# Decoder step on one core: the bias copies of heads 4 to 7 tied to attention's first four stores instead of the sixth projection chunk's

## The chip, the cores and the metric

The kernel runs on one core of one Trainium2 chip. The metric is the device time of one execution in microseconds (us). The engines are TensorE (PE, with its weight loads shown as PEld), VectorE (DVE), ScalarE (ACT), GpSimd (POOL) and SyncE (SP, which here only issues transfers).

## The reference

One inference step of a hybrid decoder: a state-space branch beside sparse attention with a relative-position bias, then a mixture of 32 experts of which each token takes four. There are 1024 prompt tokens and eight sample tokens, the latter with a paged cache of 4096 positions each. The part around the change is attention:

```python
def nsa_core(q, gates, q_pos, ckv, gather_fn, n_blocks, wkv, w_pos, table):
    ...
    o_cmp, p_cmp = attend_compressed(qh, ckv, q_pos, table)
    idx, valid = select_blocks(p_cmp, q_pos, n_blocks)
    o_sel = attend_selected(qh, gather_fn(idx), idx, valid, q_pos, table)
    o_win = attend_window(qh, wkv, q_pos, w_pos, table)
    ...
    g = jax.nn.sigmoid(gates.astype(F32)).astype(o.dtype)
    return jnp.einsum('bqhdr,bqhr->bqhd', o, g).reshape(B, Tq, D_ATT)
```

Each of the three branches adds to its scores a bias that depends on the head and on the distance of query and key only (`shared_bias`: `table[rel_bucket(dist)]`), and takes a softmax. A query block is 128 prompt tokens; eight heads share two key/value heads, four to each.

## The kernel before

**Stages.** `run` (L2293) goes through adaLN, preparation of the state-space branch and the bias, then `mixer_x` (normalised input), `mixer` (input projection with the state-space branch beside it), `attention`, `post` (output projection, router), `dispatch`, `experts` and `combine`. All weights are split into a high and a low part, so a product is three matmuls (L476 to L478).

**Projection.** `mixer` loads `w_in` in seven chunks of columns (a = 0, 256, 512, 768, 1024, 1280, 1536). For each, `w_split` (L622) loads raw weights into `wir` (L631, by SP, three buffers), ACT makes the high part `wih` (L632) and DVE the low part `wil` (L633); then come the eight sample rows and the eight token tiles t. Chunk 1024 stores `cmp_p`, chunk 1280 stores `sel_p` (both eight stores of `kv` by SP), chunk 1536 makes the windowed keys, values and gates and stores the last four tiles to `win_p` (L729).

**Bias.** `bias_prep` (L1258) leaves in DRAM the tile `bt`, 8 heads by 1152 distances. `spread_bias` copies one row of `bt` to 128 rows of `bx`, DRAM to DRAM, 576 KB for each head, issued by SP. `tc.issue_after(x)` makes the scheduler place it behind instruction x. Attention reads `bx` with a row step of 1151 elements, which gives each query row its own shift: the table `tt` (L1346), four transfers for a group of four heads, one buffer.

**Attention.** `attention` (L1319) runs over group g = 0, 1 (heads 0 to 3, then 4 to 7), for each over the eight query blocks t, up in g = 0 and down in g = 1. `soft` makes the scores of four heads into `sc` on PE (L1366 to L1383), DVE adds the bias and takes the row maximum (L1360), ACT makes the exponentials (L1390), DVE and ACT scale them (L1399, L1397). `values` transposes (L1413), splits (`th` L1416 on ACT, `tl` L1417 on DVE) and multiplies by the values (L1418, L1419) into `po`, which has one buffer; at the end DVE adds the halves into `at` (L1428, L1429) and SP stores it to `attd` (L1430). The values of one block are interleaved with the scores of the next.

**Sample chain.** The eight sample tokens' attention is a generator, `self.chain`, of which `block` takes about one step per block of values, tied with `issue_after` to that block's matmul `last`. Its first part, `sample_prep` (L1466), loads rows `hdn` (L1532), multiplies (L1534), makes compressed probabilities `pc` (L1539), picks the 15 best blocks and ends in the row numbers `rx` (L1600). Its second part, `sample_attention` (L1644), fetches cache rows `slab` by `rx` (L1661, POOL, two buffers), 16 fetches in four groups n of four. Each fetch is copied (`kw` L1668, `sv` L1679 on POOL), transposed (L1682), copied on ACT (`kt` L1687), multiplied (L1690) and added to its bias (`st` L1692 on DVE). Four of them make a group: transposed (L1697), copied to `px` (L1699), put through a softmax (L1637 to L1642, ACT L1639), transposed again (L1707, L1708) and multiplied by `sv` (L1716). `sv` and `px` have one buffer.

**What sets the order.** The Tile scheduler orders all instructions of an engine at build time, by dependencies, by the `issue_after` ties and by its own reckoning of when engines and transfers are free. On the chip each engine works through its list in that order.

Of the kernel before, what the change touches and what calls it, by code (L numbers as in the profile page):

```python
# [451 lines left out]
class K:  # L452
# [192 lines left out]
    def mixer(self, ctx):  # L645
        nc, i, o = self.nc, self.i, self.o
# [8 lines left out]
        with ExitStack() as c:  # L655
            side, early = (c.enter_context(ExitStack()) for _ in range(2))
            self.wir = self.pool("wir", ctx=early)
            self.wi[1] = self.pool("wi1", ctx=early)
            q = self.pool("miq", bufs=2, psum=True, ctx=c)
            for m, (a, n) in enumerate(((0, 256), (256, 256), (512, 256), (768, 256), (1024, 256), (1280, 256), (1536, 280))):  # L660
                hi, lo = self.w_split(self.wi[m % 2], win[:, a:a + n], n, "wi", 1, self.wir) if m else self.w0
                if a == 256:
                    steps = self.ssm(side)
                if a == 1280:
                    for _ in steps:
                        pass
                    side.close()
                    kv = self.pool("kv", ctx=ctx, side="right")
                    self.kh = kv.tile([128, 2, 2, T], FR, name="kh")
                    self.kl = kv.tile([128, 2, 2, T], FR, name="kl")  # L670
                    self.v = kv.tile([128, 2, 2, NT, 128], FR, name="v")
                if a == 1536:
                    early.close()
                    self.late = ctx.enter_context(ExitStack())
                    self.sap = self.pool("sap", ctx=self.late, side="right")
                    self.compress_prompt()
                def sample_rows():
                    po = q.tile([128, 512], F, name="po")
                    self.proj(po[:8, :n], slice(T, T + B), hi, lo, n)
                    zt = p2.tile([8, 280], F, name="zt")  # L680
                    nc.scalar.activation(out=zt[:, :n], in_=po[:8, :n], func=AF.Copy)
                    nc.sync.dma_start(out=self.zs[:, a:a + n], in_=zt[:, :n])
                    if a >= 1280:
                        nc.sync.dma_start(out=self.vnew[:, :, int(a == 1536)], in_=zt[:, 128:256].rearrange("b (h d) -> b h d", h=2))
                    if a in (1024, 1280):
                        nc.sync.dma_start(out=o["cmp_s" if a == 1024 else "sel_s"][0].rearrange("b t c h d -> (b t) (c h d)"), in_=zt[:, :256])
                    if a == 1536:
                        nc.sync.dma_start(out=self.zg, in_=zt[:, 256:280])
                        nc.sync.dma_start(out=o["win_s"][0].rearrange(wst)[:, 511], in_=zt[:, :256])
                if m:  # L690
                    sample_rows()
                for t in range(NT):
                    if 256 <= a < 1280 and t % 2:
                        next(steps, None)
                    po = q.tile([128, 512], F, name="po")
                    self.proj(po[:, :n], slice(t * 128, (t + 1) * 128), hi, lo, n)
                    rows = slice(t * 128, (t + 1) * 128)
                    flat = "o t c h d -> (o t) (c h d)"
                    if a < 512:
                        ut = p2.tile([128, 256], F, name="kv")  # L700
                        nc.scalar.activation(out=ut, in_=po[:, :256], func=AF.Copy)
                        nc.sync.dma_start(out=self.ud.rearrange("m t f -> (m t) f")[rows, a:a + 256], in_=ut)
                    elif a < 1024:
                        g = (a - 512) // 256
                        qd = p2.tile([128, 4, 2, 64], F, name="qd")
                        nc.scalar.activation(out=qd, in_=po[:, :256].rearrange("p (h d) -> p h d", h=4)[:, :, None, :].to_broadcast([128, 4, 2, 64]), func=AF.Copy, scale=0.125)
                        tp = q.tile([128, 4, 128], F, name="tp")
                        for h in range(4):
                            nc.tensor.transpose(tp[:, h], qd[:, h].rearrange("p a d -> p (a d)"), self.ident)
                        dst = self.qs[:, g * 4:g * 4 + 4, rows]  # L710
                        nc.scalar.activation(out=dst, in_=tp, func=AF.Copy)
                        nc.vector.tensor_tensor(out=dst[64:128], in0=tp[64:128], in1=dst[64:128].bitcast(F), op=ALU.subtract)
                    else:
                        if a > 1024:
                            kd = p2.tile([128, 2, 2, 64], F, name="qd")
                            nc.scalar.activation(out=kd, in_=po[:, 0:128].rearrange("p (h d) -> p h d", h=2)[:, :, None, :].to_broadcast([128, 2, 2, 64]), func=AF.Copy)
                        kv = p2.tile([128, 280], F, name="kv")
                        nc.scalar.activation(out=kv[:, :n], in_=po[:, :n], func=AF.Copy)
                        if a == 1024:
                            st = nc.sync.dma_start(out=o["cmp_p"][0].rearrange(flat)[rows], in_=kv[:, :256])  # L720
                            self.spread_bias(st, a, t)
                            continue
                        br = int(a == 1536)
                        if br == 0:
                            st = nc.sync.dma_start(out=o["sel_p"][0].rearrange(flat)[rows], in_=kv[:, :256])
                            self.spread_bias(st, a, t)
                        else:
                            if t >= 4:
                                nc.sync.dma_start(out=o["win_p"][0].rearrange(flat)[(t - 4) * 128:(t - 3) * 128], in_=kv[:, :256])  # L729
                            gv, kg = self.gate[:, t].rearrange("p (h r) -> p h r", r=3), kv[:, 256:280].rearrange("p (h r) -> p h r", r=3)  # L730
                            nc.vector.tensor_copy(out=gv[:, :, 0:2], in_=kg[:, :, 1:3])
                            nc.vector.tensor_copy(out=gv[:, :, 2:3], in_=kg[:, :, 0:1])
                        tp = q.tile([128, 4, 128], F, name="tp")
                        for h in range(2):
                            nc.tensor.transpose(tp[:, h], kd[:, h].rearrange("p a d -> p (a d)"), self.ident)
                        nc.scalar.activation(out=self.kh[:, br, :, rows], in_=tp[:, :2], func=AF.Copy)
                        nc.vector.tensor_tensor(out=self.kl[:, br, :, rows], in0=tp[:, :2], in1=self.kh[:, br, :, rows].bitcast(F), op=ALU.subtract)
                        v32 = kv[:, 128:256].rearrange("p (h d) -> p h d", h=2)
                        nc.vector.tensor_copy(out=self.v[:, br, :, t, 0:64], in_=v32)
                        nc.gpsimd.tensor_tensor(out=self.v[:, br, :, t, 64:128], in0=v32, in1=self.v[:, br, :, t, 0:64].bitcast(F), op=ALU.subtract)  # L740
                if not m:
                    sample_rows()
            self.chain = self.sample()
            next(self.chain)
            nc.scalar.activation(out=self.gate, in_=self.gate, func=AF.Sigmoid)

    def spread_bias(self, st, a, t):

        if t % 2:
            h = (a - 1024) // 64 + t // 2  # L750
            with self.tc.issue_after(st.ins):
                self.nc.sync.dma_start(out=self.bx[h:h + 1], in_=self.bt[h:h + 1, None].to_broadcast([1, 128, 1152]))


    def exp_poly(self, pool, out, x, n):
# [563 lines left out]
    def attention(self):  # L1319
        nc = self.nc  # L1320
        v, A, pe = nc.vector, nc.scalar, nc.tensor
        self.att = self.tc.dram_tile([128, 4, T], F, name="attd")
        with ExitStack() as c:
# [78 lines left out]
            def values(g, t, pr):  # L1402
                nonlocal last
                rows = slice(t * 128, (t + 1) * 128)
# [23 lines left out]
                v.tensor_tensor(out=at[lo], in0=ov[lo, :, 0], in1=sh[lo], op=ALU.add)  # L1428
                v.tensor_tensor(out=at[hi], in0=ov[hi, :, 1], in1=sh[hi], op=ALU.add)  # L1429
                self.put = nc.sync.dma_start(out=self.att[:, 2 * g:2 * g + 2, rows], in_=at).ins  # L1430

# [951 lines left out]
```

## Time and profile before

| | |
|---|---|
| median of three runs | 3181.55 us (3177.50 to 3199.51) |
| profiled execution | 3182.16 us, span 3180.5 us, mean granted PE clock 0.95 |
| PE, PEld busy | 93%, 75% of the span |
| DVE, ACT, POOL busy | 73%, 56%, 11% of the span |
| chunk 1280 and 1536 of the projection | about 578 to 655 us |
| attention | about 655 to 1067 us |

The rows shown below give the start of an instruction in us from the start of the span, its length, the engine, line and tiles, and in square brackets how long the engine was idle before it and what released it. "SPq" is an issue of a transfer by SP. A matmul is told by its records: a start to the next start is what it cost, and a wider spacing at the same shape is a lower clock. "Granted clock" (PEclk) is the share of 2.4 GHz that TensorE got.

### The profile page before, as it was taken

The page shows a single profiled execution, that of the slowest core. Times are in us where ns is not written, and L with a number is a line of the kernel's source. Part 1 is how long each engine was busy: PE and PEld are TensorE (multiplying, and loading weights), DVE is VectorE, ACT ScalarE, POOL GpSimd, SP SyncE. Part 2 cuts the span into 40 slices and gives each one's busy share as a digit, 9 for nine tenths or more (in the row PEclk, how much of TensorE's full clock was granted, in tenths as well). Part 3 has the DMA queues.
Part 4 walks back from the last instruction along what each step waited for, and adds up shares of the span by engine and source line. Part 5 has one row for each costly group of instructions (what it writes and reads, how often), then busy time and mean ns, then how long its engine had stood idle before and what let it go on. Part 6 is the DMA issues. An engine that isn't in the chain of part 4 may idle for free. (4 is left out here: it accounts for less than half of the span.)

```text
span 3180.5 us, 51086 instructions
## 1 busy us (share of the span) xinstructions
PE 2961.4 (93%) x15721; PEld 2370.0 (75%) x15722; DVE 2313.7 (73%) x4359; ACT 1793.6 (56%) x2838; POOL 359.1 (11%) x475
## 2 busy tenths in 40 slices
PE   7899899889998797699999999999999999999977
PEld 4666799767777585487888888888877888878752
DVE  5767655267778487788788868776589865796978
ACT  3434554266667353567566656654478644684751
POOL 0620211003220001000000000000000000000023
PEclk8999899988889798799999999999999999999988
DMA  8775333315331534699879869754199915792926
GB/s 291 248 254 195 91 109 110 108 52 124 89 107 41 178 117 171 239 316 308 279 261 351 296 226 334 266 189 158 53 324 372 321 52 199 252 369 86 362 78 275
DMA packets 436941, 656.09 MB, mean 206 GB/s; under 512 B 37268, under 2 KB 362884, under 8 KB 432629
## 3 DMA queue, kind: packets, MB, share of 16 engines
q1 hardware_dynamic: 402118, 528.58, 49.4%
q0 software_dynamic: 25072, 117.69, 10.8%
q10 hardware_dynamic: 9632, 8.31, 0.8%
q8 instruction: 65, 1.06, 0.1%
q14 instruction: 54, 0.44, 0.0%
HBM read 594.69 MB, written 68.73 MB: 209 GB/s over the span
## 5 line engine op out<-in xcount | busy, mean ns | idle before, releaser
L273 DVE TENSOR_TENSOR lo<-raw,hi 128x1024 fp32r<-128x1024 f32 x582 | 694.4, 1220 | 235.5 <-ACT hi L200 230.4
L200 ACT ACTIVATE hi<-raw 128x1024 fp32r<-128x1024 f32 x582 | 617.7, 1063 | 332.3 <-PE pc L389 331.0
L387 PE MATMUL pc<-hi,X 128*128 128x512 f32 x1408 | 562.6, 400 | 4.8 <-DVE X L278 3.9
L389 PE MATMUL pc<-hi,X 128*128 128x512 f32 x1408 | 552.1, 392 | 0.0
L388 PE MATMUL pc<-lo,X 128*128 128x512 f32 x1408 | 550.7, 391 | 0.0
L273 DVE TENSOR_TENSOR lo<-rawd,hi 128x1024 fp32r<-128x1024 f32 x288 | 340.0, 1219 | 72.6 <-ACT hi L200 72.6
L200 ACT ACTIVATE hi<-rawd 128x1024 fp32r<-128x1024 f32 x288 | 300.6, 1060 | 160.5 <-PE pc L389 160.5
L387 PEld LDWEIGHTS pc<-hi,X 128*128 128x128 f32 x1408 | 265.0, 188 | 62.5 <-issue 8.9
L389 PEld LDWEIGHTS pc<-hi,X 128*128 128x128 f32 x1408 | 264.7, 188 | 58.5
L388 PEld LDWEIGHTS pc<-lo,X 128*128 128x128 f32 x1408 | 265.3, 188 | 52.8
L387 PE MATMUL pc<-hi,HT 128*128 128x512 f32 x704 | 283.0, 402 | 10.0 <-DVE HT L295 9.0
L389 PE MATMUL pc<-hi,HT 128*128 128x512 f32 x704 | 275.1, 391 | 0.0
L388 PE MATMUL pc<-lo,HT 128*128 128x512 f32 x704 | 274.5, 390 | 0.0
L387 PEld LDWEIGHTS pc<-hi,HT 128*128 128x128 f32 x704 | 132.2, 188 | 49.7 <-issue 24.8
L476 PE MATMUL po<-wih,hh 128*128 128x256 f32 (+3 forms) x504 | 148.7, 296 | 9.6 <-ACT wih L632 5.9
L389 PEld LDWEIGHTS pc<-hi,HT 128*128 128x128 f32 x704 | 132.2, 188 | 28.7
L388 PEld LDWEIGHTS pc<-lo,HT 128*128 128x128 f32 x704 | 132.4, 188 | 25.1
L477 PE MATMUL po<-wil,hh 128*128 128x256 f32 (+3 forms) x504 | 147.5, 293 | 0.1
L478 PE MATMUL po<-wih,hl 128*128 128x256 f32 (+3 forms) x504 | 146.7, 291 | 0.0
L1360 DVE CUSTOM_DVE_ANT_0 pt<-sc,tt 128x512 f32<-128x512 f32 (+7 forms) x256 | 107.5, 437 | 49.2 <-PE sc L1376 24.1
L422 POOL DMA_INDIRECT xg<-hd,ic x52 | 62.9, 1210 | 590.7 <-PE px L355 559.9
L1390 ACT ACTIVATE pt<-pt,mx 128x640 f32<-128x640 f32 (+15 forms) x192 | 112.2, 589 | 9.5 <-DVE mx L1387 9.3
(710 smaller groups left out, 5879.9 us busy)
## 6 DMA issues: line engine op xcount, KB each, us to landing
raw<-in_w_gate_up_dram SPq DMA_DIRECT2D x248, 1024.0 KB, 10.1
rawd<-in_w_down_dram SPq DMA_DIRECT2D x64, 2048.0 KB
wt<-in_w_ada_dram SPq DMA_DIRECT2D x24, 1024.0 KB
yd<-yt SPq DMA_DIRECT2D x44, 512.0 KB
w<-ssmw SPq DMA_DIRECT2D x16, 512.0 KB
raw<-in_w_gate_up_dram POOLq DMA_DIRECT2D x8, 1024.0 KB, 15.5
wir<-in_w_in_dram SPq DMA_DIRECT2D x20, 256.0 KB
bx<-bt SPq DMA_DIRECT2D x8, 576.0 KB
```

The costliest lines, as they stand in the source:

```text
L200: A.activation(out=hi[:,u%H],in_=rawview(u),func=AF.Copy).then_inc(S['hi'][u],1)
L273: V.tensor_tensor(out=lo[:,u%H],in0=rawview(u),in1=hi[:,u%H].bitcast(F),op=ALU.subtract).then_inc(S['lo'][u],1)
L387: PE.matmul(o,lhsT=sH,rhs=wh,start=kt==0,stop=False)
L388: PE.matmul(o,lhsT=sH,rhs=wl,start=False,stop=False)
L389: ins=PE.matmul(o,lhsT=sL,rhs=wh,start=False,stop=kt==7)
L422: G.indirect_dma_start(out=xg,out_offset=None,in_=x,in_offset=bass.IndirectOffsetOnAxis(ap=ic[:,b:b+1],axis=0)).then_inc(S['xg'][b],16)
L476: pe.matmul(o, lhsT=lh, rhs=rh, start=start, stop=False)
L477: pe.matmul(o, lhsT=lh, rhs=rl, start=False, stop=False)
L478: return pe.matmul(o, lhsT=ll, rhs=rh, start=False, stop=stop)
L1360: v.tensor_tensor_reduce(out=pt[:, off[r] + a:off[r] + a + n], in0=sc, in1=bias, scale=1.0, scalar=-3e38, op0=ALU.add, op1=ALU.max, accum_ ...
L1390: A.activation(out=o, in_=o, func=AF.Exp, bias=mx[:, h, r:r + 1], accum_out=sm[:, h, r:r + 1])
```

## The change

Heads 0 to 3 keep their place behind the odd stores of chunk 1024. The four copies of heads 4 to 7 leave the odd stores of chunk 1280 and are tied to the stores of attention's blocks g = 0, t = 0 to 3.

```diff
                         if a == 1024:
                             st = nc.sync.dma_start(out=o["cmp_p"][0].rearrange(flat)[rows], in_=kv[:, :256])
-                            self.spread_bias(st, a, t)
+                            if t % 2:
+                                self.spread_bias(st.ins, t // 2)
                             continue
                         br = int(a == 1536)
                         if br == 0:
-                            st = nc.sync.dma_start(out=o["sel_p"][0].rearrange(flat)[rows], in_=kv[:, :256])
-                            self.spread_bias(st, a, t)
+                            nc.sync.dma_start(out=o["sel_p"][0].rearrange(flat)[rows], in_=kv[:, :256])
...
-    def spread_bias(self, st, a, t):
-
-        if t % 2:
-            h = (a - 1024) // 64 + t // 2
-            with self.tc.issue_after(st.ins):
-                self.nc.sync.dma_start(out=self.bx[h:h + 1], in_=self.bt[h:h + 1, None].to_broadcast([1, 128, 1152]))
+    def spread_bias(self, st, h):
+
+        with self.tc.issue_after(st):
+            self.nc.sync.dma_start(out=self.bx[h:h + 1], in_=self.bt[h:h + 1, None].to_broadcast([1, 128, 1152]))
...
                 self.put = nc.sync.dma_start(out=self.att[:, 2 * g:2 * g + 2, rows], in_=at).ins
+                if g == 0 and t < 4:
+                    self.spread_bias(self.put, 4 + t)
```

The instructions stay the same; their order does not. The new order differs from the old on every engine from the seventh chunk on and is the same again from a place early in attention's second group. In the changed kernel the store L725 is L726, and the old lines L747 to L1430 stand two lines higher (L752 is L750, L1419 is L1417, the store L1430 is L1428).

On SP, at the sixth chunk's stores (`kv`), the copies (`bx<-bt`) and the loads of the seventh chunk's weights (`wir`) stand so before:

```order
215 L725 DMA out_dram<-kv 128x256 x2
216 L752 DMA bx<-bt 128x1x1152
217 L725 DMA out_dram<-kv 128x256 x2
218 L752 DMA bx<-bt 128x1x1152
219 L725 DMA out_dram<-kv 128x256 x2
220 L752 DMA bx<-bt 128x1x1152
221 L725 DMA out_dram<-kv 128x256 x2
222 L752 DMA bx<-bt 128x1x1152
223 L631 DMA wir<-in_w_in_dram 128x2x280 x3
224 L1114 DMA e<-in_phi_w_dram 128x8x64 x4
```

and so in the change:

```order
215 L726 DMA out_dram<-kv 128x256 x2
216 L631 DMA wir<-in_w_in_dram 128x2x280 x2
217 L726 DMA out_dram<-kv 128x256 x2
218 L631 DMA wir<-in_w_in_dram 128x2x280
219 L726 DMA out_dram<-kv 128x256 x3
220 L1112 DMA e<-in_phi_w_dram 128x8x64
221 L726 DMA out_dram<-kv 128x256
222 L1112 DMA e<-in_phi_w_dram 128x8x64 x3
```

The weight loads moved from behind all eight stores to behind the second and the fourth.

On PE, in attention's first group, the sample chain's fourth fetch of its first group (L1682, L1690) and the transposes of its `st` (L1697) stand so before, among score and value matmuls:

```order
3184 L1682 MATMUL b<-ident,kw 128x120 x4
3185 L1373 MATMUL sc<-kh,qs 128x512
3186 L1374 MATMUL sc<-kl,qs 128x512
3187 L1418 MATMUL po<-th,v 128x512
3188 L1376 MATMUL sc<-far,eye 128x128
3189 L1690 MATMUL b<-qp,kt 120x8 x4
3190 L1419 MATMUL po<-tl,v 128x512
3191 L1418 MATMUL po<-th,v 128x512
3192 L1413 MATMUL tp<-ident,pt 128x128 x2
3193 L1419 MATMUL po<-tl,v 128x512
3194 L1697 MATMUL b<-ident,st 16x120 x4
```

and so in the change, from the third fetch on:

```order
3365 L1682 MATMUL b<-ident,kw 128x120 x4
3366 L1690 MATMUL b<-qp,kt 120x8 x4
3367 L1682 MATMUL b<-ident,kw 128x120 x4
3368 L1690 MATMUL b<-qp,kt 120x8 x4
3369 L1697 MATMUL b<-ident,st 16x120 x8
3370 L1707 MATMUL b<-ident,px 120x16 x8
3371 L1708 MATMUL b<-ident,px 16x16
3372 L1716 MATMUL b<-st,sv 64x4 x32
3373 L1682 MATMUL b<-ident,kw 128x120 x4
3374 L1690 MATMUL b<-qp,kt 120x8 x4
```

The chain moved to a later place, and no attention matmul stands between its steps there: the next three fetches and the eight L1697 of the second group follow in the same way, and then comes `L1416 MATMUL po<-th,v`, the first value matmul of t = 6.

On DVE the chain's first step after its multiplication, `pc` (L1539), stood behind the second `at` of the first group before, with nine rows of attention between; in the change it stands so, directly behind the fifth (the first piece), and the second group's softmax stands ahead of the sixth `at` (the second piece, `px` to L1427):

```order
1257 L1426 TENSOR_TENSOR at<-po,sh 64x256
1258 L1427 TENSOR_TENSOR at<-po,sh 64x256
1259 L1539 SCALAR_TENSOR_TENSOR pc<-b,qbs,bc 64x255
1260 L1542 TENSOR_REDUCE mm<-pc 64x1
1261 L1415 TENSOR_TENSOR tl<-tp,th 128x512
```

```order
1378 L1692 TENSOR_TENSOR st<-b,sb 120x8x4 x4
1379 L1699 COPY px<-b 16x480 x2
1380 L1637 TENSOR_REDUCE m_9187<-px 16x1
1381 L1638 TENSOR_SCALAR m_9187<-m_9187 16x1
1382 L1640 RECIPROCAL m_9187<-m_9187 16x1
1383 L1641 TENSOR_TENSOR m_9187<-m_9187,gate_7475 16x1
1384 L1642 TENSOR_SCALAR px<-px,m_9187 16x976
1385 L1426 TENSOR_TENSOR at<-po,sh 64x256
1386 L1427 TENSOR_TENSOR at<-po,sh 64x256
```

From the second to the fifth `at` DVE had 265 instructions before, 42 of them the chain's; the change has 285 there, none of them the chain's. On SP the four copies now follow one each behind the stores of blocks 0 to 3, and the four `tt` loads of the second group stand behind the sixth and the seventh store in place of one run of four.

## Rows read from the trace of the kernel before

**Rows 1.** The page, busy time: engine, us, share of the span, instructions.
```profile
PE 2961.4 (93%) x15721; PEld 2370.0 (75%) x15722; DVE 2313.7 (73%) x4359; ACT 1793.6 (56%) x2838; POOL 359.1 (11%) x475
```

**Rows 2.** Windows: stretch, its length, busy us of PE, PEld, DVE, ACT, POOL, clock, DMA.
```profile
692.66:781.03 88.37, 78.60 (x460) 60.40 (x458) 67.89 (x268) 53.35 (x129) 21.64 (x27) 0.85 0.36 86
658.00:850.00 192.00, 175.10 (x997) 136.03 (x997) 144.67 (x610) 123.82 (x319) 39.40 (x48) 0.84 0.35 88
```

**Rows 3.** Timeline of SP, last stores of the sixth chunk, and the first `tt`.
```profile
580.88 0.82 SPq L725 DMA_DIRECT2D out_dram<-kv  x2
...
601.30 0.48 SPq L752 DMA_DIRECT2D bx<-bt  x1
601.82 1.61 SPq L631 DMA_DIRECT2D wir<-in_w_in_dram  x3
...
652.47 0.37 SPq L729 DMA_DIRECT2D out_dram<-kv  x1
...
654.54 1.79 SPq L1346 DMA_DIRECT2D tt<-bx  x4
```

**Rows 4.** Waits from 600 to 615 us: total, times, longest.
```profile
ACT wih L632 <- DMA wir<-in_w_in_dram: 6.7, 1, 6.7
...
PE po L476 <- ACT wih L632: 5.9, 1, 5.9
```

**Rows 5.** Timeline of PE at the start of the seventh chunk.
```profile
608.09 0.64 PE L476 MATMUL po<-wih,hh 128*8 128x280 f32 x2 [5.91 <-ACT wih L632]
...
609.30 0.43 PE L476 MATMUL po<-wih,hh 128*8 128x280 f32 x1
...
612.34 0.41 PE L477 MATMUL po<-wil,hh 128*8 128x280 f32 x1
...
612.71 0.29 PE L477 MATMUL po<-wil,hh 128*128 128x280 f32 x1
612.84 0.29 PE L478 MATMUL po<-wih,hl 128*128 128x280 f32 x1
```

**Rows 6.** Timeline of DVE: `at`, `pc`, `rx` and the fifth `at`.
```profile
692.20 0.43 DVE L1429 TENSOR_TENSOR at<-po,sh 64x256 f32<-64x256 f32 x1
...
697.00 0.47 DVE L1539 SCALAR_TENSOR_TENSOR pc<-b,qbs,bc 64x255 f32<-64x255 f32 x1
...
715.38 0.17 DVE L1600 CAST rx<-b 120x32 int32<-120x32 f32 x1
...
780.60 0.43 DVE L1429 TENSOR_TENSOR at<-po,sh 64x256 f32<-64x256 f32 x1
```

**Rows 7.** Timeline of POOL: first fetch, first and fourth `kw`, second group's `sv`.
```profile
715.87 1.08 POOL L1661 DMA_INDIRECT slab<-in_cache_sel_kv_dram,rx  x1 [62.22 <-DVE mx L1360]
...
724.07 0.61 POOL L1668 COPY kw<-slab 120x512 f32<-120x512 f32 x1 [4.51 <-DMA attd<-at]
...
740.53 0.61 POOL L1668 COPY kw<-slab 120x512 f32<-120x512 f32 x1 [1.81 <-DMA slab<-in_cache_sel_kv_dram,rx]
...
772.22 1.16 POOL L1679 COPY sv<-slab 120x512 f32<-120x512 f32 x2 [23.57 <-PE b L1716]
```

**Rows 8.** The fetches of L1661, issue to landing, from that line's own view.
```profile
DMA to landing us min/median/max: 7.2/7.9/12.2
```

**Rows 9.** Timeline of DVE: fourth `st`, end of the first `px`, eighth `st`.
```profile
747.17 0.19 DVE L1692 TENSOR_TENSOR st<-b,sb 120x32 f32<-120x32 f32 x1 [0.28 <-PE b L1690]
...
756.80 0.71 DVE L1642 TENSOR_SCALAR px<-px,m 16x976 f32<-16x976 f32 x1
...
799.04 0.19 DVE L1692 TENSOR_TENSOR st<-b,sb 120x32 f32<-120x32 f32 x1 [0.39 <-PE b L1690]
```

**Rows 10.** Timeline of PE: an L1534, two L1716, the first row of the common order.
```profile
689.92 0.86 PE L1534 MATMUL b<-hdn,e 64*64 64x256 f32 x3
...
770.28 1.87 PE L1716 MATMUL b<-st,sv 120*64 120x4 f32 x16
...
880.99 1.09 PE L1716 MATMUL b<-st,sv 120*64 120x4 f32 x16
...
882.27 0.79 PE L1419 MATMUL po<-tl,cv 63*128 63x512 f32 x1
```

## The prediction

> **What bounds the kernel now.** I read the page's busy times first: PE is at work for 93% of the span [rows 1]. Nearly anything that costs time therefore has to make PE wait, and anything that gains has to take such a wait away. Next I read the windows. Attention's first group, 658 to 850 us, has 175.1 us of PE in 192, so PE is idle there for only 16.9 us, while DVE works 144.7, ACT 123.8 and POOL 39.4 [rows 2]. POOL's work, the sample chain's fetches and copies, is therefore almost wholly hidden: between those steps PE and DVE have attention to do. Then I read the timelines and waits at the two places that the new order touches.
>
> **The copies themselves.** Four issues leave chunk 1280 and four enter attention. SP issues one in about 0.5 us, and in the middle of attention (692.66 to 781.03) transfers took a share of 0.36 of the DMA engines [rows 2, 3]. The tables of the second group are needed only after eight blocks. As transfers I cost them at nothing. They are covered by that free share. Without this cover they would delay a slab or a store by their own few us.
>
> **Gain at the seventh chunk.** Before, the `wir` loads leave SP at 601.82, behind all eight stores and four copies, though the first pair of stores left at 580.88 [rows 3]. ACT waits 6.7 us for them and PE 5.9 for ACT [rows 4]. In the new order two of the three loads follow the first pair of stores and the third the next pair, so they leave roughly 18 us earlier and both waits go: −5.9. The matmuls behind the wait start 3.04/13 = 0.234 us apart (609.30 to 612.34) and then 0.13 (612.71 to 612.84) [rows 5]. Some nineteen at the lower clock cost 0.1 too much each: −1.9. The trace says that an idle stretch of 5.9 us was followed by the clock's lower level; without it the higher one should hold. What is late next is the last tile's path to `tt`, whose issue follows the last store closely (652.47, 654.54), so it moves up with PE [rows 3]. I take −8. If ACT now meets a load that has not landed, at most 1.5 is lost; if the table issue also gains, 1.5 more is won: −6 to −9.5.
>
> **Loss in attention's first group: where the chain starts.** The order puts the chain's `pc` behind the fifth `at` instead of the second. Before, the stretch from the second to the fifth took 88.4 us for 265 DVE instructions, 42 of them the chain's, and DVE was busy for 67.89 of it [rows 2, 6]. That is 0.256 us an instruction. The new stretch has 285, all attention: 285 × 0.256 = 73 us, if DVE does not wait. The nearest bounds are 66 (the small maximum rows that make up much of the difference are shorter than the mean) and 80 (DVE's idle share kept in part). So the second `at` comes at 692.2 − 8 = 684.2, the fifth at about 757. From `pc` to `rx` it took 697.00 to 715.38 = 18.4 us [rows 6]. I keep this, since less attention lies between but the round trips stay. So `rx` comes at R = 775.6 instead of 715.4, with 768 to 782 as its bounds.
>
> **Loss: what then lies bare.** Behind R, PE's list holds two groups of the chain with almost no attention between. PE works through its list in order, so it stands still at each step that is not ready. DVE has some 60 attention instructions left behind R, 14 to 18 us at 0.256 or a little less, then only the chain's steps too. I add the steps up, each from its rows:
> - The first fetch leaves 0.5 behind R and its `kw` starts 8.2 later, so R + 8.7 [rows 6, 7]. That agrees with a landing of 7.9 [rows 8].
> - The fourth `kw` comes 16.5 behind the first (724.07 to 740.53). With two slab buffers this is two landings in a row, so it doesn't shrink when the engines are free: R + 25.2. Its `st` came 6.6 later, between attention rows [rows 7, 9]; bare I take 3: R + 28.
> - `px` and its softmax took from 747.17 to 757.51, 10.3 us, with attention between; bare, the six dependent steps and their hand-overs take some 8: R + 36 [rows 9].
> - The transposes and the four L1716 steps: each of those four took 1.09 or 1.87 us, by the clock [rows 10], so 4.4 to 7.5, plus some 1.5 for L1707 and the copy behind it. I take 9, the end nearer to the lower clock, because PE has been waiting: R + 45.
> - The second group's eighth `st` came 26.8 behind its first `sv` (772.22 to 799.04) [rows 7, 9]. `sv` waits for the L1716 steps, so this cannot start before R + 45. Its first two slabs have landed by then; the other two need one landing of 7.9 behind the `sv` copies and then the steps above: I take 16, with 26.8 as the upper bound.
> - `px` again 8, the two `at` rows 0.85, and `po` is free: PE resumes attention at R + 70, that is 845.
>
> Within these 70 us PE has little more to do than the chain's own steps, of which the L1716 of two groups (8.7 to 15) are the largest, so I estimate some 22 us of work and 48 of waiting, against 16.9 of waiting in the whole group before.
>
> **From there to the common order.** 301 of PE's instructions lie between that place and the row that stood at 882.27 before. Before, the 888 from 689.92 to there took 192.4 us, 0.217 each [rows 10]. At that pace 301 need 65 us; without the idle share (175.1/192) 59. They now hold two of the chain's groups fewer to wait for: 58.5. So this row comes at 845 + 58.5 = 903.5 instead of 882.27: **+21**, with the gain of 8 already in it. Behind it both orders are the same, so the rest moves as it stands: 3182.16 + 21 = 3203 us. The profiled execution is 0.6 us above the median of 3181.55, so against the median I say 3202.5.
>
> **A rule beside it.** The Trainium skill, page "TensorE: Matmul & The Clock Gate", Part 1, states that an array that has idled runs at 1.2 GHz until it has been busy for a while. By it the whole bare stretch would run at the lower level, also the matmuls right behind it. The trace agrees in kind (the rows behind the 5.9 us wait), and shows both prices for one step. By the rule alone the sum would be the upper one, the second rival below.
>
> **Rivals.**
> (1) *The bare steps are no longer than before, only elsewhere, or the engines find attention to do in between.* DVE's leftover and PE's remaining scores would then fill the gaps, and only the first gain is left: 3182 − 8 = 3174. The prices of the chain speak against it: R + 70 has two fetch series that no engine can shorten, and PE's list has no attention to put between. It decides if R comes 20 us earlier than I say, that is if the stretch of 285 takes 53 instead of 73.
> (2) *The bare groups are as slow as the rows of before*, because the chain's own hand-overs and the lower clock set them and not the attention between: 6.6 instead of 3, 10.3 twice instead of 8, 26.8 instead of 16. That adds 3.6 + 4.6 + 10.8 = 19: 3202.5 + 19 = 3221.5, or 3230 if the 301 instructions behind also run at 0.217 and R is 2 later. The clock of 0.84 in that stretch [rows 2] speaks for it; the slab landing, which no attention row lengthens, speaks against it for the 26.8.
> (3) *The move changes nothing that can be measured*: the gain of 8 and a smaller loss cancel, 3178 to 3187. For this the chain would have to lose only one fetch series (16.5 us) to the bare stretch and the second be overlapped; the `sv` buffer speaks against it.
>
> **How the numbers follow.** Forecast 0.55, with its own range 3188 to 3213; rival (1) 0.12; rival (2) 0.25; rival (3) 0.08. A difference of 1% (31.8 us) is about what a measurement of this kernel can tell from no change. Faster by that much (below 3150) none of them reaches; I leave 0.02. Slower by it (above 3213) is all of (2) and a little of the forecast's upper end: 0.27. Within: 0.71. The range from 3177 to 3228 leaves out (1) and the end of (2), together no more than 0.2.
>
> **What would show each step.** In the changed profile the waits at the seventh chunk must lack PE's 5.9 for ACT. On DVE `pc` should stand near 757 and `rx` near 775. PE's window from about 795 to 845 should show it idle for more than half, released by DVE's `px`, ACT's `kt` and the slab landings behind them, and the row L1417 `po<-tl,cv` should come near 903. I am wrong if PE is busy there above 80%; if `rx` comes before 760; or if the copies in attention delay slabs or stores, which would show as fetches that land beyond 12 us.

## The result, and the profile after

| | before | change |
|---|---|---|
| median | 3188.0 us (3177.5 to 3199.5, four runs) | 3228.0 us (3224.7 to 3229.4, four runs) |
| ratio | | 1.0114, 95% interval 1.0082 to 1.0146 |
| profiled execution | 3182.2 us, span 3180.5, clock 0.950 | 3227.7 us, span 3226.1, clock 0.942 |

The change makes the kernel slower by 1.1%, 36 us by the ratio. The forecast was 3202.5 within 3177 to 3228, so the sign was right, the measured median lies at the range's very end, and the likeliest value was some 25 us too low; by the ratio, which makes the loss 36 us where the forecast had 21, it was some 15 too low.

SP in the change, timeline at the sixth chunk's stores and at the first `tt` (start, length, line):

```profile
589.12 1.00 SPq L631 DMA_DIRECT2D wir<-in_w_in_dram  x2
591.43 0.42 SPq L631 DMA_DIRECT2D wir<-in_w_in_dram  x1
...
649.04 1.82 SPq L1344 DMA_DIRECT2D tt<-bx  x4
```

The weight loads leave 10 to 13 us earlier on the clock of the trace than the 601.82 of [rows 3], and 18 to 20 earlier when the 7.4 us are taken off by which this execution was already late (below). The window over the start of the seventh chunk, which holds the 5.9 us wait of [rows 4] in the kernel before, is now full (columns as in [rows 2]):

```profile
600.00:612.00 12.00, 11.90 (x94) 10.26 (x92) 1.54 (x8) 3.16 (x9) 1.05 (x3) 1.00 0.58 139
```

DVE in the change, timeline: the second and the fifth `at` (L1427 here), `pc`, `rx`, fourth and eighth `st`, the two `px`, and the sixth `at`. These answer [rows 6] and [rows 9]:

```profile
686.23 0.43 DVE L1427 TENSOR_TENSOR at<-po,sh 64x256 f32<-64x256 f32 x1
...
766.83 0.43 DVE L1427 TENSOR_TENSOR at<-po,sh 64x256 f32<-64x256 f32 x1
767.28 0.47 DVE L1539 SCALAR_TENSOR_TENSOR pc<-b,qbs,bc 64x255 f32<-64x255 f32 x1
...
785.47 0.19 DVE L1600 CAST rx<-b 120x32 int32<-120x32 f32 x1
...
814.48 0.19 DVE L1692 TENSOR_TENSOR st<-b,sb 120x32 f32<-120x32 f32 x1 [4.48 <-PE b L1690]
...
821.09 0.71 DVE L1642 TENSOR_SCALAR px<-px,m 16x976 f32<-16x976 f32 x1
...
830.38 0.17 DVE L1718 COPY os<-b 64x16 f32<-64x16 f32 x1 [7.25 <-PE b L1716]
...
847.93 0.19 DVE L1692 TENSOR_TENSOR st<-b,sb 120x32 f32<-120x32 f32 x1 [4.31 <-PE b L1690]
...
854.53 0.71 DVE L1642 TENSOR_SCALAR px<-px,m 16x976 f32<-16x976 f32 x1
855.60 0.43 DVE L1427 TENSOR_TENSOR at<-po,sh 64x256 f32<-64x256 f32 x1
```

POOL and PE in the change: the first `kw`, the fourth fetch and its `kw`; the late multiplication of `hdn`, the resumption of attention behind the sixth `at`, and the first row of the common order. They answer [rows 7] and [rows 10]:

```profile
794.55 0.61 POOL L1668 COPY kw<-slab 120x512 f32<-120x512 f32 x1 [4.89 <-DMA slab<-in_cache_sel_kv_dram,rx]
...
801.64 1.12 POOL L1661 DMA_INDIRECT slab<-in_cache_sel_kv_dram,rx  x1 [0.29 <-POOL sv L1679]
...
810.23 0.61 POOL L1668 COPY kw<-slab 120x512 f32<-120x512 f32 x1 [0.65 <-DMA slab<-in_cache_sel_kv_dram,rx]
```

```profile
762.37 3.66 PE L1534 MATMUL b<-hdn,e 64*64 64x256 f32 x16
...
856.08 0.79 PE L1416 MATMUL po<-th,v 128*128 128x512 f32 x1 [5.23 <-DVE at L1427]
...
916.51 0.49 PE L1417 MATMUL po<-tl,cv 63*128 63x512 f32 x1
```

And the windows of the change over these stretches: the stretch from the second to the fifth `at`, the bare steps in two halves, and what follows.

```profile
686.70:767.30 80.60, 67.82 (x348) 48.53 (x346) 68.34 (x285) 62.86 (x149) 0.00 (x0) 0.95 0.12 34
...
785.50:822.00 36.50, 23.70 (x114) 17.30 (x115) 20.77 (x75) 15.83 (x34) 18.02 (x21) 0.66 0.70 165
822.00:856.00 34.00, 21.11 (x129) 17.90 (x129) 5.43 (x15) 3.81 (x8) 12.77 (x16) 0.50 0.51 118
856.00:918.00 62.00, 60.05 (x392) 47.84 (x393) 35.37 (x112) 30.42 (x66) 14.11 (x19) 0.83 0.39 103
```

Up to 801 us PE still has 12.5 us of attention's matmuls, scores above all, between the chain's; from there to 856 it has the chain alone. In the second half DVE has 5.4 us of work in 34 and ACT 3.8, and the granted clock is 0.50, the lower of its two levels (1.2 of 2.4 GHz). Who waits for whom there (total, times, longest):

```profile
DVE st L1692 <- PE b L1690: 25.2, 7, 5.0
ACT kt L1687 <- PE b L1682: 24.6, 5, 8.5
POOL kw L1668 <- DMA slab<-in_cache_sel_kv_dram,rx: 16.6, 7, 4.9
...
PE b L1690 <- ACT kt L1687: 7.4, 7, 3.0
...
PE b L1707 <- DVE px L1642: 4.5, 1, 4.5
```

Each engine waits for the other: this is a chain run by itself. No copy leaves beside it; SP in the change, the last of the four, 48 us ahead of `rx`:

```profile
737.49 0.49 SPq L750 DMA_DIRECT2D bx<-bt  x1
```

The two parts of attention as windows, from the second `at` to the row of the common order and from there to the last `at`, the first of them before and in the change, the second before:

```profile
692.20:882.27 190.07, 173.53 (x1061) 137.17 (x1059) 142.40 (x536) 117.48 (x269) 44.15 (x54) 0.86 0.37 90
686.23:916.51 230.28, 186.65 (x1056) 141.75 (x1054) 146.00 (x532) 120.69 (x270) 43.58 (x54) 0.81 0.34 84
882.27:1066.77 184.50, 167.36 (x1074) 134.68 (x1073) 131.38 (x519) 123.17 (x319) 25.46 (x41) 0.88 0.26 79
```

Read whole, the profiled execution is 45.6 us longer in span. Of these, 7.4 were there already at 570 us, before any row of the order differs (the same transfers of the projection are 7.4 later in one trace than in the other); −13.3 come at the last two chunks, counted up to the second `at`; +40.2 between the second `at` and the common row (190.1 to 230.3); +13.0 between there and the last `at`; and −1.7 in the output projection.

### The profile page after: what moved, and what is told of

Read it like the earlier page. It is cut to its first block, busy times and chain, and to the rows that moved or that the text cites. A ratio compares the mean times of both kernels' runs of the same rounds, so it can differ in the third digit from the quotient of the medians.

```text
span 3226.1 us, 51113 instructions
## 1 busy us (share of the span) xinstructions
PE 2983.5 (92%) x15721; PEld 2385.0 (74%) x15722; DVE 2319.5 (72%) x4359; ACT 1796.5 (56%) x2838; POOL 357.3 (11%) x475
## 5 line engine op out<-in xcount | busy, mean ns | idle before, releaser
L389 PEld LDWEIGHTS pc<-hi,X 128*128 128x128 f32 x1408 | 264.6, 188 | 58.5
L387 PEld LDWEIGHTS pc<-hi,HT 128*128 128x128 f32 x704 | 132.2, 188 | 49.6 <-issue 24.8
L388 PEld LDWEIGHTS pc<-lo,HT 128*128 128x128 f32 x704 | 132.4, 188 | 25.2
L1358 DVE CUSTOM_DVE_ANT_0 pt<-sc,tt 128x512 f32<-128x512 f32 (+7 forms) x256 | 107.2, 437 | 29.8 <-PE sc L1374 15.7
L1414 ACT ACTIVATE th<-tp 128x512 fp32r<-128x512 f32 (+5 forms) x148 | 83.7, 590 | 71.1 <-PE tp L1411 56.4
```

Source lines behind the costliest of these rows:

```text
L387: PE.matmul(o,lhsT=sH,rhs=wh,start=kt==0,stop=False)
L388: PE.matmul(o,lhsT=sH,rhs=wl,start=False,stop=False)
L389: ins=PE.matmul(o,lhsT=sL,rhs=wh,start=False,stop=kt==7)
L1358: v.tensor_tensor_reduce(out=pt[:, off[r] + a:off[r] + a + n], in0=sc, in1=bias, scale=1.0, scalar=-3e38, op0=ALU.add, op1=ALU.max, accum_ ...
L1414: A.activation(out=th[:n], in_=tp[:n], func=AF.Copy)
```

## The experiments

Two theories stood against each other. *Order*: the loss is the sample chain's late and bare place, which the scheduler chose; the copies cost nothing as transfers. *Transfers*: 576 KB copies in SP's queue hold up what attention needs.

| run | what | median us | ratio to before, 95% interval |
|---|---|---|---|
| e1 | copies at blocks 1 to 4 | 3208.7 | 1.0047 (1.0028 to 1.0067) |
| e2 | `hdn` loads by ACT | 3203.0 | 1.0049 (1.0030 to 1.0068) |
| e3 | no copies of heads 4 to 7 | 3175.5 | 0.9965 (0.9941 to 0.9988) |
| e4 | copies at blocks 0, 1, 4, 5 | 3228.8 | 1.0136 (1.0113 to 1.0158) |
| e5 | copies behind the last `hdn` loads | 3199.8 | 1.0031 (1.0009 to 1.0053) |
| e6 | all eight copies at chunk 1024 | 3208.1 | 1.0064 (1.0042 to 1.0085) |
| e7 | copies at the `win_p` stores | 3187.8 | 0.9995 (0.9977 to 1.0014) |
| e8 | the change again | 3224.9 | 1.0105 (1.0068 to 1.0141) |
| e9 | copies at tiles 4 to 7 of chunk 1280 | 3196.3 | 1.0012 (0.9993 to 1.0030) |
| e10, e11 | the kernel before, profiled again | 3182.4, 3200.5 | |
| e12 | copies of heads 4 to 7 issued by ACT | 3192.9 | 1.0011 (0.9990 to 1.0032) |

The kernel before ran beside them, with medians of 3185.6 (e1 to e4), 3188.6 (e5 to e8), 3191.9 (e9 to e11) and 3190.4 us (e12). The ratio is not the quotient of the medians; it differs from it most in e1, whose eleven runs spread from 3187 to 3214. Distances below go by the ratio.

**e1, one block later.**

```diff
-                if g == 0 and t < 4:
-                    self.spread_bias(self.put, 4 + t)
+                if g == 0 and 1 <= t < 5:
+                    self.spread_bias(self.put, 4 + t - 1)
```

> The four copies stay in attention but are tied to the stores of blocks 1 to 4 instead of 0 to 3. By the order of this kernel the sample chain's pc then stands behind the second at again, and the weight loads of the seventh chunk keep their early place. Theory 'order' (the loss is the chain's late place and its bare steps, the copies cost nothing as transfers): the loss is gone and the gain at the seventh chunk is left, 8 to 13 us below the kernel before. Theory 'transfers' (576 KB copies in SP's queue hold up stores, hdn loads or slab fetches in attention): the four copies are still there, so still 25 to 40 us above the kernel before.

**e3, no copies of these heads.**

```diff
-                    h0 = self.bx[4 * g:4 * g + 1]
+                    h0 = self.bx[0:1]
...
-                if g == 0 and t < 4:
-                    self.spread_bias(self.put, 4 + t)
```

> The copies of heads 4 to 7 are left out altogether; the second group reads the tables of heads 0 to 3 (so its bias is that of other heads; the work is the same). Order as in e1. Theory 'order': the same as e1 within 4 us, 8 to 13 below the kernel before. Theory 'transfers': 8 to 13 below the kernel before too, but 35 to 50 below e1.

e3 came out 11 us below before, which both theories had said of it. e1 lies 15 above (the medians lie 23 apart), between the two forecasts, and so does its distance of 26 from e3. The totals alone would have spoken for 'transfers', since copies seemed to cost 26. The traces say otherwise. Up to the end of the first `px` e1 and e3 have the same order on every engine but for the copies on SP, and in that stretch e1 issues three copies that e3 doesn't have, so it measures the copies by themselves. SP in e1, and then the same stretch, from the second `at` to the end of L1642, in e1 and in e3:

```profile
689.80 0.53 SPq L750 DMA_DIRECT2D bx<-bt  x1
...
715.58 0.49 SPq L750 DMA_DIRECT2D bx<-bt  x1
...
742.16 0.47 SPq L750 DMA_DIRECT2D bx<-bt  x1
```

```profile
688.91:753.80 64.89, 56.48 (x332) 43.26 (x330) 56.55 (x225) 44.58 (x107) 17.52 (x21) 0.92 0.50 127
```

```profile
680.34:745.96 65.62, 56.57 (x332) 43.28 (x330) 57.66 (x225) 44.65 (x107) 17.55 (x21) 0.92 0.42 98
```

The same 332 PE records and 225 of DVE take 64.9 us with three copies beside them and 65.6 without. What shows of them is the DMA share, 0.50 against 0.42. The difference in total begins only behind this stretch, where e1's order leaves that of e3 (the fifth `at` stands behind two more score steps of DVE there, and one group of the chain is pushed behind it). So moving the first copy one block back removed the chain's late start but not every displacement: the expectation of e1 took "pc behind the second at" for the whole order, and that was wrong.

**e2, the change with `hdn` on another queue.**

```diff
-            nc.sync.dma_start(out=hdn.rearrange("p (b h) n -> p b h n", h=2), in_=self.hdn[0:64, b:b + 2])
+            nc.scalar.dma_start(out=hdn.rearrange("p (b h) n -> p b h n", h=2), in_=self.hdn[0:64, b:b + 2])
```

> The change as it is, with the copies behind the same four stores, but the hdn loads are issued by ACT instead of SP. The order then has the chain early again (pc behind the second at). Theory 'order': 8 to 13 us below the kernel before, perhaps 1 less for ACT's issues. Theory 'transfers': as the change, 30 to 40 us above the kernel before, since each copy leaves at the same store.

The copies leave at the same four stores as in the change (671 to 751 us), and the loss falls from 1.1% to 0.5%. By these two numbers some half of it therefore hung on one thing: that the scheduler saw the last `hdn` loads behind two copies in SP's queue. On the chip they were not late: the change issues them at 687.7 and PE multiplies them only at 762.4, where its order has them. What is left in e2 I put down to displacement again. PE waited there four times for `at`, in the window 683 to 892 us, against once for 0.6 us in the kernel before (658 to 850 us):

```profile
PE po L1416 <- DVE at L1427: 15.1, 4, 5.2
```

**e4 and e5, other places in attention.** e4 ties the copies to blocks 0, 1, 4 and 5:

```diff
-                if g == 0 and t < 4:
-                    self.spread_bias(self.put, 4 + t)
+                if g == 0 and t in (0, 1, 4, 5):
+                    self.spread_bias(self.put, (0, 1, 4, 5).index(t) + 4)
```

> Copies tied to the stores of blocks 0, 1, 4 and 5, so only two of them stand ahead of the last hdn loads. By the order the chain's pc again stands behind the fifth at, but its groups lie elsewhere: the long run of 154 chain matmuls without attention comes with the second and third group, behind the seventh at. Theory 'order': slower than the kernel before by 15 to 45 us, since a late start and a bare run are both there. Theory 'transfers': half of the copies ahead of hdn, so about half the loss of the change, and no waits of PE for the chain's own steps.

It is as slow as the change. `pc` comes at 762.8, behind the fifth `at`, and from there to 900 us, where three groups of the chain lie, PE is busy for 107.8 of 137.6 us at a clock of 0.69. That is what 'order' expects of a late start, and not half the loss. Up to the fifth `at` e4 has the order of the change on PE, DVE and ACT, but one copy between the second and the fifth (682.6) where the change has three (687.1, 702.6 and 737.5). The stretch takes 80.6 us in both; e4:

```profile
681.75:762.37 80.62, 68.28 (x350) 48.84 (x348) 68.37 (x284) 63.31 (x149) 0.00 (x0) 0.96 0.08 19
```

e5 leaves all four copies in attention, but behind the last `hdn` loads:

```diff
+            if b == B - 2:
+                for z in range(4):
+                    self.spread_bias(hl, 4 + z)
...
-                if g == 0 and t < 4:
-                    self.spread_bias(self.put, 4 + t)
```

Here `hl` is the load of `hdn`.

> All four copies of heads 4 to 7 stay in attention, issued by SP behind the last hdn loads (between the stores of blocks 0 and 3), so about 680 to 745 us. The order has the chain's pc behind the second at, and on PE no run of the chain longer than 32 matmuls. Theory 'order': the gain at the seventh chunk is left, 5 to 12 us below the kernel before. Theory 'transfers' (copies inside attention cost time whatever the order, which would explain why e1 and e2 lie 26 us above e3): 10 to 20 us above the kernel before, like e1 and e2.

Ten us above before: 'order' was wrong by 15 to 22, and the total lies at the lower end of what 'transfers' forecast. The trace decides between them. All four copies leave between 680.5 and 685.5 us, around the second `at`, and from there up to e3's fourth `at` PE, DVE, ACT and POOL work through the same order in both runs. This stretch in e5 and then in e3:

```profile
682.81:735.31 52.50, 44.89 (x257) 34.10 (x256) 44.87 (x182) 33.42 (x82) 16.03 (x19) 0.90 0.54 142
```

```profile
680.34:733.03 52.69, 44.77 (x257) 34.12 (x256) 45.47 (x182) 33.42 (x82) 15.94 (x19) 0.90 0.42 101
```

With four copies just issued it takes 52.5 us, without any 52.7. Then the orders part: in e3 the fourth `at` follows at 733.5, in e5 only at 753.6. PE waited twice for `at` (9.1 us), and the first part of attention took 203.6 us, against 187.5 in e3. So it is where the order puts the steps and not the presence of the copies. A chain whose start is in place is not yet an undisturbed order.

**e6, e7, e9, e12: copies outside attention.** e6 ties heads 4 to 7 to the even stores of chunk 1024, e7 to the four `win_p` stores, e9 to tiles 4 to 7 of chunk 1280, e12 issues them from ACT's queue:

```diff
-            self.nc.sync.dma_start(out=self.bx[h:h + 1], in_=self.bt[h:h + 1, None].to_broadcast([1, 128, 1152]))
+            (self.nc.scalar if h > 3 else self.nc.sync).dma_start(out=self.bx[h:h + 1], in_=self.bt[h:h + 1, None].to_broadcast([1, 128, 1152]))
```

> All eight copies are tied to the stores of chunk 1024 (heads 4 to 7 to its even ones), so neither chunk 1280 nor attention has any; from the seventh chunk's weight loads on, the order is that of e3. Both theories: 6 to 12 us below the kernel before, if the wait for weights is gone and doesn't come back at chunk 1280; if the eight copies now delay chunk 1280's loads as four of them did those of the seventh, the gain is lost and it is within 3 us of the kernel before.

> The copies are tied to the four win_p stores of the seventh chunk, ahead of the first group's table loads in SP's queue. PE's order is word for word that of e3. This measures the copies as transfers where they stand ahead of something attention waits for. Theory 'order': the gain of e3, less what the copies delay the four table loads: 0 to 10 us, so between 12 below the kernel before and equal to it. Theory 'transfers': the price of four copies, 20 us or more above e3.

> The copies of heads 4 to 7 stay at chunk 1280 but are tied to its stores of tiles 4 to 7 instead of the odd tiles 1, 3, 5, 7. The order then issues the seventh chunk's weight loads ahead of all but one store tied to a copy, and from early in the seventh chunk on PE's order is that of e3 and of the kernel before. Theory 'order': the wait of 5.9 us at the seventh chunk is gone and attention is untouched: 5 to 12 us below the kernel before, as e3. Theory 'transfers': the copies lie outside attention, so the same; it differs only if the copies hold up the last stores and the table loads: then within 5 us of the kernel before.

> A version that could beat both kernels: the copies of heads 4 to 7 are issued by ACT, on whose queue the tie to an SP store does not bind, so they leave as soon as the bias row is in DRAM (during adaLN, some 300 us ahead of the projection). From the projection on, all engines' order is that of e3, with no copy at chunk 1280 or in attention of these heads; ahead of it the order of adaLN and compression differs in some 500 PE instructions. If that part takes as long as before: 8 to 13 us below the kernel before, as e3. If the four transfers or the other order there cost time (adaLN is loading weights), the gain is lost: within 5 us of it or above.

In all four the first part of attention takes 184 to 191 us, as in before: their order leaves it alone. None beats the kernel before. e6, the only one clearly slower, missed both forecasts: eight copies at chunk 1024 lie in front of the state-space branch's weights, and PE waits for those, from 555 to 640 us:

```profile
PE sp L1029 <- DMA w<-ssmw: 11.5, 2, 7.8
```

It has lost 27 us against e3 by the seventh chunk and no more than the clock's share behind it. Of the 27, 11.5 are this wait, 5.9 another for the next projection weights, and some 10 come from the clock: the same 422 matmul records from 528 us on take 59.9 us at 0.78, against 49.9 at 0.97 in e3. In e7, whose order on PE is that of e3, DVE waits 7.9 us for the tables, against 3.9 in e3; it comes out equal to the kernel before, at the end of what 'order' allowed it, and some 10 us above e3, where 'transfers' had forecast 20 or more. e9 has its weights in time, but from 600 to 640 us PE is busy for 34.2 of 40 where e3 has 39.9; there the loads for the prompt's compression stand behind the copies and the order differs from both kernels, and which of the two costs it wasn't followed up. e12 loses some 20 us between 243 and 382 us, in adaLN and what follows it, where its four copies leave (238 to 276) and its order differs, on PE up to 332 and on ACT up to 385; which of the two costs it stays open too. So a copy can cost something as a transfer where it stands ahead of a load with a waiter, as in e6 and e7 and in the kernel before at the seventh chunk; in attention it was not seen to.

**e8, e10, e11: what the second part of attention costs.** The change again, and twice more the kernel before, for the 13 us behind the common row.

> The change as it is, on the same chip and beside the same runs of the kernel before as e5 to e7. Expected again 30 to 45 us above the kernel before. Its profile is read for two things: whether the second group of attention, whose order is that of the kernel before, again takes some 11 us longer than in the kernel before, and at which granted clock.

> The kernel before, profiled once more. Read for one thing: how long attention takes from the first row of the common order to the last at. It was 184.5 us at a granted clock of 0.88 in the first profile of the kernel before, while the same instructions in the same order took 192 to 199.5 at 0.78 to 0.82 in the change, e3, e6 and e7. If the 184.5 was one execution's luck this profile shows 190 to 200; if the change itself lengthens that part, it shows 184 to 187 again.

> As e10, a further profile of the kernel before, for the same question: 190 to 200 us for the second part of attention if 184.5 was luck, 184 to 187 if the change is what lengthens it.

From the common row to the last `at`, the same instructions in the same order on all engines:

| profile | us | granted clock |
|---|---|---|
| before, e10, e12 | 184.5, 184.1, 184.4 | 0.88 |
| e3, e9, e5 | 191.9, 192.3, 193.2 | 0.82 |
| e6, e7, the change, e8, e2 | 199.3, 199.5, 197.5, 196.8, 197.6 | 0.78, 0.78, 0.79, 0.81, 0.80 |
| e11 (before) | 200.1 | 0.78 |

The third profile of the kernel before, from its common row on:

```profile
886.49:1086.55 200.06, 185.84 (x1074) 149.92 (x1073) 131.47 (x519) 123.91 (x319) 25.54 (x41) 0.78 0.25 73
```

The kernel before takes 184 or 200 us for it, by the execution. The distance is not spread over the part: 13.6 of the 15.6 us lie in two of its eight blocks. The first of them, from the second to the third `at` behind the common row, and the other, up to the last `at` but one, in the first profile of before and in the third:

```profile
914.96:950.99 36.03, 32.00 (x226) 26.57 (x226) 25.04 (x96) 22.71 (x51) 11.51 (x15) 0.91 0.47 158
1046.21:1061.69 15.48, 14.18 (x109) 10.26 (x107) 6.60 (x13) 6.11 (x15) 1.65 (x3) 0.72 0.20 60
```

```profile
919.47:962.70 43.23, 40.80 (x226) 33.77 (x226) 24.55 (x96) 23.07 (x51) 11.50 (x15) 0.68 0.40 131
1059.58:1081.51 21.93, 20.66 (x117) 15.59 (x116) 6.69 (x12) 6.33 (x15) 1.65 (x3) 0.50 0.15 43
```

DVE and ACT have almost the same work there in both; PE's takes longer at the lower clock. e3 is slow in the first of these blocks alone (43.1 and 15.9 us), the change in both (42.2 and 21.9). The 13 us are therefore not shown to be the change's: one kernel shows as much between two executions, and the profile on which the sum was made was one of the quick ones. That no profile of the change shows the quick value doesn't settle it, with two against three. The first part, in contrast, took 190.1, 186.8 and 183.3 us in three profiles of before and 230.3 and 233.5 in two of the change. By their means it costs 45 us; less the gain of 11 to 13 that is some 33 of the 36 to 40 us between the medians, so most of the loss is there, whatever the second part does.

## Why the prediction came out as it did

| step | predicted | change | e8 |
|---|---|---|---|
| gain up to the second `at` | −8 | −13.3 | −10.6 |
| second to fifth `at` | 73 | 80.6 | 80.6 |
| `pc` to `rx` | 18.4 | 18.2 | 18.3 |
| `rx` to PE's resumption | 70 | 70.6 | 73.3 |
| resumption to the common row | 58.5 | 60.4 | 60.7 |
| behind the common row | 0 | +11 | +11 |

The gains are counted without the 7.4 us (7.8 in e8) by which these executions were late before any order differed.

**The mechanism was right, and it is the order.** `pc` came directly behind the fifth `at`, and PE and DVE did two groups of the chain with almost nothing between. The steps came where they were put: fourth `kw` at R + 24.8 (25.2), its `st` at R + 29 (28), end of `px` at R + 36.3 (36), end of the first group's L1716 at R + 44.9 (45), eighth `st` 17.5 behind it (16). That nothing shortens the first series of fetches held: 15.7 us from the first `kw` to the fourth, against 16.5 before. But it is not two landings in a row, as I had read it: POOL's own copies and issues fill the 7.1 us up to the issue of the fourth fetch (794.55 to 801.64), and one landing the 8.6 behind it.

**The copies as transfers: right for attention.** That they cost nothing there is shown by three pairs of the same order: e1 against e3 over 65 us, e5 against e3 over 52 with all four copies, and e4 against the change over 80.6. The sign that I named against it, fetches that land beyond 12 us, did not appear: in e8, the second profile of the change, the view of L1661 that [rows 8] shows for before reads

```profile
DMA to landing us min/median/max: 7.5/8.0/11.7
```

It does not hold in general, as e6 shows.

**The clock.** The forecast split the 70 us into 22 of work and 48 of waiting; PE was busy for 44.8 and idle for 25.7. The total was right because the steps depend on one another, but the sign I named, PE idle for more than half, did not appear. Two things were wrong in the 22: I had left out the 12.5 us of attention that PE still had up to 801, and the chain's own matmuls took 33.4 us, at a clock of 0.66 and then 0.50, although the L1716 steps of one group alone lie there (7.0 us) and not of two. The 9 us that I took for those steps and what stands around them, near the lower clock, fits: 822 to 830. The Trainium skill's page "TensorE: Matmul & The Clock Gate", Part 1, says that an array that idles runs at 1.2 GHz. The trace agrees in kind: the clock is 0.50 of 2.4 GHz from 822 to 856, where PE is idle for 12.9 of 34 us.

**The stretch from the second to the fifth `at` was mis-sized by 7.6.** I put 285 instructions at DVE's busy share and let it not wait. DVE's work was even a little less, 68.3 us; but it was idle for 12.3, since ACT, PE and DVE wait for one another in attention also where no chain lies between: DVE waited 9.1 us for ACT's `th` and `pt` there, and PE 4.8 for `at`. The bound of 80 was the value.

**The gain was mis-sized by 3 to 5.** The wait and the half-clock matmuls made up some 8; e3 against before shows about 2.5 more already at the end of chunk 1280, before the wait, where the orders already differ (on ACT from 587 us on), and 1.6 behind it. I had looked at the one wait and not at the stores and loads around it.

**The reference for the sum.** I measured the sum from one execution of before, 3182 us, and its second part ran at the higher clock. Runs of before range from 3174 to 3203, with medians of 3186 to 3192 beside the experiments. The step "behind it both orders are the same, so the rest moves as it stands" holds for the order and not for the time of one execution: up to 16 us lie in that part alone between two executions of one kernel. With the 7.4 us ahead of any difference it is most of the distance that is left between the forecast and the profiled execution (7.4 and 11 of 25); whether a part of it belongs to the change can't be settled by two profiles of it.

**The rivals.** (1), the chain hidden, was wrong: 40 us were lost in the first part. (2) has about the right total, but not by its mechanism: the bare groups were as fast as forecast. (3) was wrong.

## What to carry to other kernels

Where a scheduler lays out the queues from its own reckoning of transfers, a copy put into a queue moves everything whose load stands behind it: compare the order of the two builds on all engines before costing the copy. Two groups of this chain of small dependent steps were almost hidden between other work and made the first part of attention 40 to 45 us longer where they stood by themselves, so first ask what the order leaves between its steps. And before a few us are explained, profile the kernel before twice.

## What the runs showed of the hardware that I had not expected

The same instructions in the same order took from 184 to 200 us over one part of attention, at mean granted clocks from 0.88 to 0.78, in different executions of one kernel. Most of it came in two blocks that took 36.0 or 43.2 us and 15.5 or 21.9, at clocks of 0.91 or 0.68 and 0.72 or 0.50, while the three blocks behind the first of them took 83.3 and 83.8. Also before any order differs the start of the program came out in different lengths: at 570 us executions of this kernel and its variants lay up to 11 us apart.
